# Queries, keys and the two merge gates of a transformer layer: seven products of quadrants in the input projection instead of eight, with the gates taken out of the attention loop

## The chip, the core and the metric

The kernel runs on one core of a Trainium2 chip. A core has TensorE (PE in the profile: matmuls and transposes into PSUM), VectorE (DVE), ScalarE (ACT), GpSimd (POOL) and SyncE (SP), which issues most of the loads; ScalarE issues most of the stores. Each engine executes its own instructions in the order in which the program was scheduled and waits on semaphores for the others. The metric is device time of one execution in microseconds. Three executions of the kernel before took 2883.06 us in the median (2879.89 to 2885.41).

## What is computed

One layer over 1024 tokens of width 1024, with 256 context tokens, all in float32. This is the part that matters here:

```
p  = (x * (1 + sc1) + sh1) @ w_in              # 1024 x 1024  @  1024 x 11264
qr, kr, vr, gr, qd, kd, vd, gate_r, gate_d = split(p)
qr, kr, qd, kd = rope(qr), rope(kr), rope(qd), rope(kd)
y_ret = retention_readout(retention(qr, kr, vr), gr) @ w_ret_out
y_dif = diff_readout(diff_attention(qd, kd + context, vd + context)) @ w_diff_out
y_mix = (sigmoid(gate_r + b) * y_ret + sigmoid(gate_d + b) * y_dif) @ w_o
x     = layer_norm(alpha * x + g1 * y_mix)
... conv feed-forward, layer_norm
```

The four of `qr`, `kr`, `qd`, `kd` are 1024 columns each; `gate_r` and `gate_d` (the merge's two gates) are 1024 columns each; `gr`, the retention's own gate, is 2048. `kr` and `kd` are also computed for the context tokens. `diff_attention` has eight heads, two softmaxes each.

## The kernel before, in words

**Numbers.** Every float32 operand is split into a high part `h` (a cast to the rounded format fp32r on ScalarE) and a low part `l` (the rest, a subtraction on VectorE): `split`, line 84. A product of two such operands is three matmuls, h·h, h·l and l·h (`mm3`, line 245), each 128 x 128 weights against up to 512 columns. Weights come in through a ring of tiles (`load_split`, `w_cols`): raw, then `wh` and `wl`.

**Projection.** The modulated input lies transposed in SBUF as `xH`, `xL` (8 row blocks of 128 by 1024 tokens). `qd`, `kd`, `vd`, `qr`, `kr`, `vr` are produced in that order. For queries and keys one tile is 256 weight columns, that is two halves of 128 (`proj_dif`, `proj_ret`): each half is 8 row blocks x 3 matmuls x 2 cuts of 512 tokens = 48 matmuls, so 96 per tile (`proj_T`), and for keys another 24 of 256 columns per half for the context (`pcx`). There are 16 such tiles, 4 each of `qd`, `kd`, `qr`, `kr`; the first is done with the two halves side by side while the input is still being prepared (`proj_first`). The two halves are the pair that the rotary embedding combines: four multiplications from PSUM on VectorE, one subtraction and one addition on GpSimd (`rope`). For `qd` and `kd` the result is split again and goes to memory in 16 pieces of 32 partitions, issued by ScalarE. `vd` and `vr` are produced the other way round (tokens on partitions, `proj_N`).

**Attention.** 64 steps, one for each head and block of 128 queries (`steps`). Each step has two scores (`score`): 6 matmuls into the one PSUM tile `sp` (bufs=1), a scan on VectorE that scales, copies and takes the maximum (line 720), and an exponential on ScalarE. `combine` joins the two on VectorE (line 77), `flip` transposes the result on TensorE (`tp`, ten transposes) and splits it (`ath`, `atl`), and `avd` multiplies by the values every second step (`po`, 30 matmuls). Since `sp` is one tile, the next score cannot start before the scan of the last one has ended. Between the scores the generator `gates` (line 677) puts in work that depends on none of this: the projections of `gr` and of the two merge gates, 32 blocks of 128 columns, 48 matmuls each (`pg`), handed out in quarters of 12 matmuls. One quarter follows every score but the last of every sixteenth step (line 801); what remains is done after the last score.

**After it.** Retention, the merge (which reads the gates from `d_ga`), the output projection, the feed-forward network. The first of its two large products, `w_up`, is already done with seven products of quadrants in place of eight: 84 matmuls and their sums for each `f` (`first_products`, `product`, the loop at line 1350). The order of all instructions on each engine is set by a scheduler, which starts from the order of the program.

## Time and profile before

| | |
|---|---|
| median of three executions | 2883.06 us |
| the profiled execution | 2888.07 us, its span 2886.3 us |
| TensorE busy | 2793.8 us (97% of the span), 13610 matmuls |
| VectorE busy | 1626.6 us (56%) |
| ScalarE busy | 1122.6 us (39%) |
| GpSimd busy | 809.8 us (28%) |
| moved by DMA | 340 MB, mean 118 GB/s |

The profiled execution lies 5 us over the median. Busy matmuls overlap in the profile (a 512-column matmul shows 0.39 us, the next one starts 0.23 us after it), so the pace of TensorE is read from starts, or from the chain that ended last. That chain is 81% TensorE; the largest of its parts are `pg` (18%), `pxn` (11%) and `px` (11%). The granted TensorE clock is full nearly throughout.

### The profile page before, as it was taken

The numbers are of one execution on the slowest core, as the hardware profiler recorded it, in microseconds if no ns is written. First come the engines' busy times: TensorE is split into PE (matmuls) and PEld (weight loads), VectorE is DVE, ScalarE is ACT, GpSimd is POOL, SyncE is SP. The second block draws the span as 40 slices with busy tenths as digits, with TensorE's granted clock in tenths as the row PEclk, the third lists the DMA queues.
The fourth block names the chain that finished last, engine by engine and source line by source line (L and its number), as shares of the span: only waits on it lengthen the run. The fifth ranks groups of instructions, "written<-read, shape, count | busy, mean of one in ns | idle before, by whom it ended". The sixth has DMA issues, their size and how long they took to land.

```text
span 2886.3 us, 34740 instructions
## 1 busy us (share of the span) xinstructions
PE 2793.8 (97%) x13610; PEld 2327.8 (81%) x13610; DVE 1626.6 (56%) x2139; ACT 1122.6 (39%) x1570; POOL 809.8 (28%) x613
## 2 busy tenths in 40 slices
PE   7999999999999999999998999899998999999997
PEld 5888888888788888888886877788776788888876
DVE  4864243322167766777758775333556555557666
ACT  4321211111144545544546767433345444444221
POOL 3321022100000000000027764234442333337744
PEclk9999999999999999999999999999999999999999
DMA  8755332453233332323233433643321322224421
GB/s 250 212 165 168 125 124 79 132 175 110 70 92 92 112 95 93 108 91 103 65 113 107 140 115 113 236 150 120 118 89 52 110 81 88 81 81 168 138 95 59
DMA packets 261476, 340.18 MB, mean 118 GB/s; under 512 B 15479, under 2 KB 192064, under 8 KB 261312
## 3 DMA queue, kind: packets, MB, share of 16 engines
q1 hardware_dynamic: 222992, 258.50, 28.7%
q10 hardware_dynamic: 38320, 79.46, 7.8%
q8 instruction: 107, 1.75, 0.3%
q14 instruction: 57, 0.47, 0.1%
HBM read 242.73 MB, written 95.17 MB: 117 GB/s over the span
## 4 chain that ended last, share of the span: by engine, by line
PE 81%; DMA 5%; DVE 5%; POOL 3%; ACT 3%; issue 3%; SPq 0%; ACTq 0%; DVEq 0%; POOLq 0%
PE pg L253 18%; PE pxn L253 11%; PE px L253 11%; PE pu L253 8%; PE py L253 8%; PE pyd L253 6%; PE sp L717 5%; PE po L253 4%; PE pxo L253 2%; PE tp L741 2%; PE pcx L253 2%; DMA g<-d_gT 1%; DVE acc L71 1%; PE pS L253 1%; DMA wraw<-in_w_in 1%
## 5 line engine op out<-in xcount | busy, mean ns | idle before, releaser
L71 DVE TENSOR_TENSOR wl<-wraw,wh 128x1024 fp32r<-128x1024 f32 (+1 forms) x233 | 319.8, 1386 | 248.1 <-ACT wh L85 241.5
L85 ACT CAST wh<-wraw 128x1024 fp32r<-128x1024 f32 (+1 forms) x233 | 218.7, 947 | 473.0 <-PE pu L253 107.9
L71 POOL TENSOR_TENSOR rd<-ident,wh 128x512 fp32r<-128x512 f32 x16 | 18.2, 1137 | 860.6 <-ACT wh L85 827.0
L720 DVE TENSOR_SCALAR_CACHE_REDUCE e<-sp 128x1280 f32<-128x1280 f32 x128 | 190.5, 1489 | 107.2 <-PE sp L717 106.5
L82 ACT ACTIVATE e<-e,m 128x1280 f32<-128x1280 f32 x128 | 175.0, 1367 | 184.0 <-DVE e L720 183.6
L71 POOL TENSOR_TENSOR wraw<-wraw 128x512 f32<-128x512 f32 x85 | 148.9, 1752 | 266.7 <-DVE wl L71 254.3
L71 POOL TENSOR_TENSOR rp<-rp,rp 128x1024 f32<-128x1024 f32 x32 | 89.0, 2804 | 379.4 <-DVE rp L71 359.7
L253 PE MATMUL pg<-xH,wh 128*128 128x512 f32 x496 | 194.9, 393 | 0.0
L253 PE MATMUL pg<-xH,wl 128*128 128x512 f32 x496 | 194.7, 393 | 0.0
L253 PE MATMUL pg<-xL,wh 128*128 128x512 f32 x496 | 194.4, 392 | 0.0
L717 PE MATMUL sp<-ks,qd 128*128 128x512 f32 (+1 forms) x768 | 174.4, 362 | 1.5 <-DVE e L720 1.4
L253 PE MATMUL py<-opH,wh 128*128 128x512 f32 x384 | 150.9, 398 | 10.0 <-DVE ga L71 6.0
L253 PE MATMUL px<-xL,wh 128*128 128x512 f32 x512 | 158.2, 390 | 0.0
L253 PE MATMUL px<-xH,wl 128*128 128x512 f32 x512 | 157.7, 389 | 0.0
L253 PE MATMUL px<-xH,wh 128*128 128x512 f32 x512 | 156.8, 391 | 0.0
L253 PE MATMUL py<-opL,wh 128*128 128x512 f32 x384 | 152.1, 396 | 1.0 <-DVE opL L71 1.0
L253 PE MATMUL pxn<-wh,xH 128*128 128x512 f32 x384 | 151.1, 394 | 0.0
L253 PE MATMUL py<-opH,wl 128*128 128x512 f32 x384 | 150.8, 394 | 0.0
L253 PE MATMUL pxn<-wh,xL 128*128 128x512 f32 x384 | 149.6, 390 | 0.0
L253 PE MATMUL pxn<-wl,xH 128*128 128x512 f32 x384 | 149.4, 389 | 0.0
L717 PEld LDWEIGHTS sp<-ks,qd 128*128 128x128 f32 x768 | 129.3, 188 | 24.6 <-DVE e L720 4.2
L81 ACT ACTIVATE st<-pxn 128x1024 f32<-128x1024 f32 x30 | 30.8, 1027 | 235.0 <-PE pxn L253 231.0
(356 smaller groups left out, 7166.7 us busy)
## 6 DMA issues: line engine op xcount, KB each, us to landing
wraw<-in_w_in SPq DMA_DIRECT2D x88, 512.0 KB
wraw<-in_w_up SPq DMA_DIRECT2D x44, 512.0 KB
mr<-in_w_mod SPq DMA_DIRECT2D x32, 512.0 KB
qd<-d_qd SPq DMA_DIRECT2D x128, 128.0 KB
ga<-d_ga SPq DMA_DIRECT2D x24, 512.0 KB
d_u<-u SPq DMA_DIRECT2D x22, 512.0 KB
fl<-d_u SPq DMA_DIRECT2D x22, 512.0 KB
wraw<-in_w_down SPq DMA_DIRECT2D x22, 512.0 KB
```

The costliest lines, as they stand in the source:

```text
L71: eng.tensor_tensor(out=o, in0=a, in1=b, op=op)
L81: return S.activation(out=o, in_=a, func=func, bias=bias, scale=scale)
L82: return S.activation(out=o, in_=a, func=func, bias=bias, scale=scale, accum_out=accum)
L85: S.copy(out=h, in_=x)
L253: PE.matmul(ps[:, c:e], w, m[:, c:e], start=start and i == 0, stop=stop and i == 2, skip_group_check=more)
L717: st["pe"] = PE.matmul(sp[:, a:b], w, r["k"][c][:, a:b], start=part == 0, stop=part == 1).ins
L720: V.tensor_scalar(out=e, in0=sp[:, :TK], scalar1=-0.125, scalar2=None, op0=ALU.mult, op1=ALU.min, accum_out=m)
L741: PE.transpose(tp[:, k, :], a[:, k * P:(k + 1) * P], ident)
```

## The change

24 column tiles of 256 (the 16 of queries and keys, and 8 for the two merge gates) are laid out as 2 x 2 quadrants: weights by the two halves of the rows and the two halves of 128 columns, input by the two halves of the rows and the two halves of the tokens. Winograd's form of Strassen's scheme gives the tile with seven products of 4 row blocks x 3 matmuls instead of eight, 84 matmuls instead of 96. The first tile of `qd` keeps the old form, so 23 tiles have the new one. For this

- sums of the input's quadrants are made once, in float32, and split: three new pairs of operands (`xs`), and one that takes the place of a quadrant of `xH`/`xL`, whose old content is stored to memory (`d_a21`, 2 MB for both) and read back for `vd`;
- sums of the weights' quadrants are made for each tile on GpSimd (four subtractions of 128 x 512), and four tiles are split instead of two (`weights_1` to `weights_3`);
- results are put together in SBUF: four copies from PSUM on ScalarE and three additions on VectorE for each tile (`proj_pair`). The rotary multiplications read from SBUF afterwards;
- the context parts of `kd` are split and sent on their own, so a key tile of `kd` has 32 pieces to send instead of 16;
- `gates` in the attention loop has 16 blocks (`gr`) instead of 32, and a quarter follows only the first score of a step, and not in steps 7, 11 and 15 of 16. 53 quarters lie in the loop or ahead of it, 11 after the last score;
- the ring of weights has 4 pairs instead of 6, and `decays` (the small tables of the retention) moves from the second query tile to the start of `vd`.

```
-    open_ring("wring1", 3, 6)
+    open_ring("wring1", 3, 4)
...
+            if k < 4:
+                continue
+            j = k - 4
+            a11, a12, a21, a22 = xn[:, j, t_lo], xn[:, k, t_lo], xn[:, j, t_hi], xn[:, k, t_hi]
+            tt(a11, a11, a21, ALU.subtract, G)
+            split(xs[7][0][:, j, :], xs[7][1][:, j, :], a11)
+            tt(a21, a21, a22, ALU.add)
+            tt(a22, a22, a11, ALU.subtract)
+            split(xs[6][0][:, j, :], xs[6][1][:, j, :], a22)
+            tt(a12, a12, a22, ALU.subtract, G)
+            split(xs[3][0][:, j, :], xs[3][1][:, j, :], a12)
...
+        def rope(pa, pb):
+            u, v = [rp.tile([P, T], F32R, name="rt%d" % i, tag="rt%d" % i, bufs=2) for i in range(2)]
+            t0, t1, p0, p1 = [x.bitcast(F32) for x in (u, v, pa, pb)]
+            tt(t0, p0, trig["cos"], ALU.mult)
+            tt(t1, p1, trig["sin"], ALU.mult)
+            tt(p0, p0, trig["sin"], ALU.mult)
+            tt(p1, p1, trig["cos"], ALU.mult)
+            tt(t0, t0, t1, ALU.subtract, G)
+            tt(p0, p0, p1, ALU.add, G)
...
+        def weights_1(f):
...
+            W[f] = {"raw": raw, "h0": ring_split(raw[0], perm, None if ctx else (0,))}
+            tt(b11, b12, b11, ALU.subtract, G)
+            tt(b12, b22, b12, ALU.subtract, G)
+        def weights_2(f):
...
+            W[f]["h1"] = ring_split(raw[1], perm)
+            tt(b22, b22, in_order(raw[0], perm, 0), ALU.subtract, G)
+            tt(b21, b21, b22, ALU.subtract, G)
+            W[f]["t0"] = ring_split(raw[0], perm)
+        def weights_3(f):
+            W[f]["t1"] = ring_split(W[f]["raw"][1], todo[f][1])
...
+        def product(ps, f, n, first):
+            w, at = W[f][places[n][0]], places[n][1]
+            for k in range(4):
+                mm3(ps, [x[:, at + k * P:at + k * P + P] for x in w], operand(n, k), 512, first and k == 0, k == 3, more=not first)
+        def proj_pair(f):
...
+            product(chain, f, 1, True)
+            S.copy(out=a[:, t_lo], in_=chain)
+            product(p2, f, 2, True)
+            tt(a[:, t_lo], a[:, t_lo], p2, ALU.add)
+            product(chain, f, 6, False)
+            S.copy(out=b[:, t_lo], in_=chain)
+            product(p5, f, 5, True)
+            S.copy(out=b[:, t_hi], in_=p5)
+            product(chain, f, 7, False)
+            tt(b[:, t_hi], b[:, t_hi], chain, ALU.add)
+            if f + 1 < len(todo):
+                weights_1(f + 1)
+            product(p5, f, 3, False)
+            tt(b[:, t_lo], b[:, t_lo], p5, ALU.add)
...
+            product(chain, f, 4, False)
+            S.copy(out=a[:, t_hi], in_=chain)
...
+        rot, todo = todo[1:] + ret, todo[:1]
+        for i, x in enumerate(rot):
+            todo.append(x)
+            if gat and i % 2 == (i > 6):
+                todo.append(gat.pop(0))
...
-            todo += [(C_GA + i * P, d_ga[i // 8, i % 8]) for i in range(16)]
...
-                    if c == 0 or n % 16 != 15:
+                    if c == 0 and n % 16 not in (7, 11, 15):
```

TensorE in the attention loop, before, at the second half of a step: `sp` are the score's matmuls, `tp` the transposes, `pg` the gate's matmuls.

```order
L717 MATMUL sp<-ks,qd 128x512 x2
L717 MATMUL sp<-ks,qd 128x256
L717 MATMUL sp<-ks,qd 128x512 x2
L717 MATMUL sp<-ks,qd 128x256
L741 MATMUL tp<-ident,e 128x128 x10
L253 MATMUL pg<-xH,wh 128x512
L253 MATMUL pg<-xL,wh 128x512
L253 MATMUL pg<-xH,wl 128x512
L253 MATMUL pg<-xH,wh 128x512
L253 MATMUL pg<-xL,wh 128x512
L253 MATMUL pg<-xH,wl 128x512
L253 MATMUL pg<-xH,wh 128x512
```

The same engine in the changed kernel, at one of the steps without a quarter:

```order
L878 MATMUL tp<-ident,e 128x128 x10
L854 MATMUL sp<-ks,qd 128x512 x2
L854 MATMUL sp<-ks,qd 128x256
L854 MATMUL sp<-ks,qd 128x512 x2
L854 MATMUL sp<-ks,qd 128x256
L854 MATMUL sp<-ks,qd 128x512 x2
L854 MATMUL sp<-ks,qd 128x256
L854 MATMUL sp<-ks,qd 128x512 x2
L854 MATMUL sp<-ks,qd 128x256
L878 MATMUL tp<-ident,e 128x128 x10
L854 MATMUL sp<-ks,qd 128x512 x2
L854 MATMUL sp<-ks,qd 128x256
```

Here two scores follow each other with nothing between, and ten transposes stand alone between the next two.

ScalarE at two key tiles of `kd`, before: `dh` and `rp` are the high and low parts that are sent, `wh` the cast of weights.

```order
L85 CAST dh<-pcx 128x256
L85 CAST wh<-wraw 128x1024 x2
L85 CAST dh<-rp_1670 128x1024
L85 CAST dh<-pcx 128x256
L497 DMA d_kd<-dh 32x1280 x2
L497 DMA d_kd<-rp_1670 32x1280 x2
L497 DMA d_kd<-dh 32x1280
L497 DMA d_kd<-rp_1670 32x1280
L497 DMA d_kd<-dh 32x1280
L497 DMA d_kd<-rp_1670 32x1280
L85 CAST dh<-rp_1672 128x1024
L497 DMA d_kd<-dh 32x1280 x3
```

ScalarE at such a tile in the changed kernel; `pa`, `pb` are the tiles in which the result is put together, `cl`, `ch` the context's.

```order
L589 COPY pa<-px 128x512
L85 CAST wh<-wraw 128x512 x2
L85 CAST rt_1954<-rt_1953 128x1024
L593 COPY pb<-px 128x512
L497 DMA d_kd<-rt_1954 32x1024 x3
L497 DMA d_kd<-rt_1953 32x1024 x3
L497 DMA d_kd<-rt_1954 32x1024
L497 DMA d_kd<-rt_1953 32x1024
L85 CAST pb<-pa 128x1024
L595 COPY pb<-pg 128x512
L497 DMA d_kd<-pb 32x1024 x3
L497 DMA d_kd<-pa 32x1024 x3
```

Copies that TensorE's next products wait for now stand between the sends on this queue.

## Rows read from the trace of the kernel before

**Rows 1.** Engines by stage: start, queries/keys of retention, attention, the handover to retention.

```profile
core 0: us, PE busy (x) PEld busy (x) DVE busy (x) ACT busy (x) POOL busy (x), PEclk, DMA share, GB/s
0.00:86.60 86.60, 66.02 (x407) 50.29 (x408) 47.55 (x102) 34.35 (x54) 33.44 (x52) 0.98 0.79 239
359.40:556.80 197.40, 197.40 (x962) 167.25 (x962) 75.73 (x58) 19.97 (x25) 41.63 (x15) 1.00 0.29 98
787.00:1474.00 687.00, 684.77 (x3901) 595.30 (x3901) 480.64 (x716) 344.62 (x476) 16.08 (x14) 1.00 0.30 93
1474.00:1560.00 86.00, 72.59 (x347) 60.33 (x346) 60.37 (x88) 43.19 (x72) 54.17 (x34) 0.88 0.39 123
```

**Rows 2.** Chain that ended last (start, us, what): key tiles in the projection.

```profile
161.18 2.87 PE pcx L253 x24
164.05 10.91 PE px L253 x48
```

**Rows 3.** The same chain, two successive `f` of the product with `w_up`.

```profile
2409.62 5.06 PE pu L253 x22
...
2428.91 5.06 PE pu L253 x22
```

**Rows 4.** TensorE in the attention loop, in order of time (start, us, ...).

```profile
1004.42 1.25 PE L741 MATMUL tp<-ident,e 128*128 128x128 f32 x10
1005.43 1.41 PE L717 MATMUL sp<-ks,qd 128*128 128x512 f32 x6
1006.68 0.39 PE L253 MATMUL pg<-xH,wh 128*128 128x512 f32 x1
...
1009.43 0.28 PE L253 MATMUL po<-ath,vh 128*128 128x256 f32 x1
...
1013.02 1.32 PE L717 MATMUL sp<-ks,qd 128*128 128x512 f32 x6
1014.18 0.40 PE L253 MATMUL pg<-xH,wh 128*128 128x512 f32 x1
```

**Rows 5.** VectorE in the attention loop: the first and the last scan.

```profile
787.08 1.48 DVE L720 TENSOR_SCALAR_CACHE_REDUCE e<-sp 128x1280 f32<-128x1280 f32 x1
...
1474.06 1.49 DVE L720 TENSOR_SCALAR_CACHE_REDUCE e<-sp 128x1280 f32<-128x1280 f32 x1 [0.64 <-PE sp L717]
```

**Rows 6.** VectorE within a step (in brackets: idle before, and what ended it).

```profile
1019.44 1.22 DVE L71 TENSOR_TENSOR wl<-wraw,wh 128x1024 fp32r<-128x1024 f32 x1
...
1029.93 0.16 DVE L732 RECIPROCAL f<-s 128x1 f32<-128x1 f32 x1 [1.52 <-ACT e L82]
...
1030.43 1.55 DVE L77 SCALAR_TENSOR_TENSOR e<-e,f 128x1280 f32<-128x1280 f32 x1
1031.92 1.49 DVE L720 TENSOR_SCALAR_CACHE_REDUCE e<-sp 128x1280 f32<-128x1280 f32 x1
...
1033.34 1.49 DVE L71 TENSOR_TENSOR atl<-tp,ath 128x1280 fp32r<-128x1280 f32 x1
```

**Rows 7.** Who waited for whom from 787 to 1474 (us, times, longest).

```profile
DVE e L720 <- PE sp L717: 105.9, 68, 4.5
...
PE sp L717 <- DVE e L720: 1.4, 1, 1.4
```

**Rows 8.** TensorE after the last score.

```profile
1489.24 0.38 PE L253 MATMUL po<-ath,vh 128*128 128x256 f32 x1 [1.31 <-ACT ath L85]
...
1491.12 1.08 PE L854 MATMUL pt<-ident,kraw 128*128 128x128 f32 x4 [1.50 <-DMA kraw<-d_kr]
```

**Rows 9.** TensorE's busy time and granted clock in two stretches of the handover.

```profile
1490.00:1500.00 10.00, 8.88 (x45) 0.66 0.82 245
1520.00:1530.00 10.00, 7.02 (x34) 0.72 0.47 143
```

**Rows 10.** GpSimd and VectorE: two of each at once in the projection, and GpSimd elsewhere.

```profile
217.64 5.76 POOL L71 TENSOR_TENSOR rp<-rp,rp 128x1024 f32<-128x1024 f32 x2 [21.81 <-DVE rp L71]
...
218.72 5.75 DVE L71 TENSOR_TENSOR wl<-wraw,wh 128x1024 fp32r<-128x1024 f32 x2
...
2036.32 2.40 POOL L71 TENSOR_TENSOR wraw<-wraw,mrow 128x1024 f32<-128x1024 f32 x1 [7.02 <-issue]
...
2318.82 2.68 POOL L71 TENSOR_TENSOR wraw<-wraw 128x512 f32<-128x512 f32 x2 [4.53 <-DVE wl L71]
```

**Rows 11.** ScalarE's queue in the projection: three sends of a key tile.

```profile
202.75 1.26 ACTq L497 DMA_DIRECT2D d_kd<-dh  x3
```

More of the change, by code (lines that the diff above doesn't have):

```diff
@@ L435, in build @@
     with ExitStack() as ph:
[L436 to L438 removed]
+        wp = wp1
         trig = {}
@@ L481, in proj_dif @@
[L481 to L493 removed]
+            return px
@@ new lines, in build, with ring_split @@
+        W = {}
+        def ring_split(raw, perm, only=None):
+            pair = [ring["pool"].tile([P, 1024], F32R, name="w" + n, tag="w" + n, bufs=ring["bufs"]) for n in "hl"]
+            if perm or only is not None:
+                for s in range(2) if only is None else only:
+                    c = slice(512 * s, 512 * s + 512)
+                    split(as_raw(pair[0][:, c], perm), as_raw(pair[1][:, c], perm), in_order(raw, perm, s))
+            else:
+                v = raw.rearrange("p (a s c) -> p s a c", a=4, s=2)
+                split(*[x.rearrange("p (s a c) -> p s a c", s=2, a=4) for x in pair], v)
+            return pair
@@ new lines, in build @@
+        rot, todo = todo[1:] + ret, todo[:1]
[3 more added lines that the diff above has]
+                todo.append(gat.pop(0))
+        first = proj_first(ws0)
+        with tc.issue_after(turns["mod"]):
+            weights_1(1)
+            weights_2(1)
+            weights_3(1)
+        for i, x in enumerate((xH, xL)):
+            ST.dma_start(out=d_a21[i], in_=x[:, 0:4, t_hi].bitcast(F32))
+        for k in range(4):
+            split(xH[:, k, t_hi], xL[:, k, t_hi], xn[:, k, t_hi])
@@ L627, in build @@
+        p0x.close()
+        ropex = ExitStack()
+        rp = ropex.enter_context(tc.tile_pool(name="rope", bufs=1, side="right"))
         with tc.issue_after(turns["mod"]):
             trig_tables("dif")
-        for g in range(4):
-            with tc.issue_after(turns["mod"]) if g == 1 else ExitStack():
-                proj_dif(C_QD, g, d_qd, False)
-            if g == 0:
-                with tc.issue_after(turns["mod"]):
-                    context()
-            if g == 1:
-                decays()
@@ L637, in build @@
-        for g in range(4):
-            proj_dif(C_KD, g, d_kd, True)
+        pair0 = out_tiles()
+        for o, p in zip(pair0, first):
+            S.copy(out=o.bitcast(F32), in_=p)
+        finish_dif(0, d_qd, pair0, None)
+        for f in range(1, len(todo)):
+            if todo[f][0] == C_QR:
+                trig_tables("ret")
+            proj_pair(f)
+            if f == 2:
+                context()
+        for i, x in enumerate((xH, xL)):
+            SP.dma_start(out=x[:, 0:4, t_hi].bitcast(F32), in_=d_a21[i])
```

160 lines of the change are left out of this document (98 added, 62 removed).

## The prediction

> **What bounds the kernel now.** I read the engines by stage first, then the chain that ended last, then the order of time on TensorE and VectorE inside the attention loop. In queries and keys TensorE is busy for all of 197.4 us, and in the attention loop for 684.8 of 687.0 us [rows 1]. The chain there is one matmul after the other: 48 of 512 columns in 10.91 us, 0.2273 us each, and 2.87 us for the 24 of a context part [rows 2]. So TensorE's pace sets the time in both stages that the change touches, and fewer matmuls count in full only where nothing else takes TensorE's place. In queries and keys VectorE is at 38% and ScalarE at 10%, so there is room. In the loop VectorE is busy for 480.6 us of 687 [rows 1], and while TensorE waits for its scan 1.4 us in all, VectorE waits 105.9 us for scores [rows 7]. The gate quarters are what keeps TensorE full there: each is 2.75 us (1006.68 to 1009.43) between scores of 1.16 us (1013.02 to 1014.18) [rows 4].
>
> **The change, part by part.** All sums are made against the profiled execution (2888.07 us, its span 2886.3) and then put on the median, which is 5 us lower.
>
> *Rotary tiles.* A tile costs 96 x 0.2273 = 21.82 us now. What 84 matmuls of the new form cost is in the trace: the product with w_up has the same seven products with the same copies and additions, and its period is 2428.91 - 2409.62 = 19.29 us [rows 3]. That is 2.53 us less, and 15 tiles have it: -38.0 us. The context parts stay as they are.
>
> *Gates in the projection.* Eight tiles of 19.29 us are new there: +154.3 us.
>
> *Gates out of the loop.* 16 blocks of 48 matmuls leave it, 64 quarters. At 2.75 us that would be 176 us, if TensorE stayed the bound, but it doesn't. I took the order of the changed kernel and went through the 127 intervals between one score and the next, on TensorE and VectorE, with durations from [rows 4, 6]: a score 1.16 us, a quarter 2.75, ten transposes 1.01 (1004.42 to 1005.43), thirty value matmuls 3.59 (1009.43 to 1013.02); a scan 1.42 (1031.92 to 1033.34), the combination 1.49 and 0.5 for its factor (1029.93 to 1031.92), the split of the transposed tile 1.4 to 1.5, of weights 1.22, and 0.2 to 1.0 for the small steps of values and read-out. An interval lasts as long as the longer of the two, and never less than a scan and a score in turn, 2.85 us, since the scores share one PSUM tile. For the order of before this gives 692 us (97 intervals by TensorE, 30 by VectorE). The trace has 1474.06 - 787.08 = 687.0 us [rows 5], so the accounting holds within 1%. For the order of the changed kernel it gives 576 us: 52 intervals are set by TensorE (270 us), 72 by VectorE (298 us, in which TensorE has 199 us of work), 3 by the pair of scan and score. TensorE's own sum is 474 us, VectorE's 478: nearly equal, and because each waits for the other at every score, the sum of the longer ones is 100 us above either. 75 intervals have no quarter; 48 of them have less than 2.85 us of work for TensorE, mostly just ten transposes. The loop shortens by 687 - 576 = 111 us, not by 176: -111.
>
> *The rest of the gates.* 11 quarters stand after the last score, 3 before the change: 8 x 2.75 = +22.0 us. They cover the waits of 1.31 and 1.50 us there [rows 8] and some of the time at a lower clock behind them (0.66 from 1490 to 1500 [rows 9]): -4. Together +18.
>
> *The start.* The input's sums add 12 casts, 20 VectorE and 8 GpSimd operations of 512 columns before the first new tile, and 2 MB are stored (8 to 9 us of transfer at 239 GB/s) where DMA is already 79% busy. TensorE has 66.0 of 86.6 us of work there, VectorE 47.6, GpSimd 33.4 [rows 1]. Most of it fits beside the loads. Between -2 and +15, I take +4. The read-back of 2 MB stands ahead of one weight load on SyncE's queue, but waits only for the fifth product of the last tile, with some 11 us of matmuls behind it: 0.
>
> *Waits in the new tiles.* Each tile has four copies and three additions that the product after next needs, so an engine that is late by more than 2.7 us stops TensorE. A rotary tile of `qd` has about ten VectorE operations with both operands in SBUF (1.22 us each) and 10 us on GpSimd: four of 128 x 512 (2.68 for two) and two of 128 x 1024 (2.40 each) [rows 6, 10]. Two such operations of each, side by side, took from 217.64 to 224.47, 6.8 us, where one after the other they need 7.2 [rows 10]. They hardly overlap. So the two engines need about 24 us for a `qd` tile, 22 for a `qr` tile and 12 for a gate tile, against 19.3 on TensorE (25 for keys); two rotary tiles and a gate tile come to 60 against 58. And ScalarE issues 32 sends per `kd` tile at 0.42 us [rows 11], between copies that TensorE waits for. In the w_up stage none of this shows, because there VectorE multiplies nothing for the rotation. Between 0 and +40, I take +12, half a microsecond a tile, nearer to the w_up row than to the full serial sum because the scheduler puts context matmuls into the gaps.
>
> The Trainium skill (SBUF — State Buffer, section "Who interferes with whom") says that a VectorE instruction with two SBUF inputs and a GpSimd instruction that reads SBUF exclude each other for the whole instruction. The 6.8 us agree with it. It speaks against the change, since the rotary multiplications read PSUM before and SBUF after; by it alone the sum would be the rival below on the projection.
>
> *The clock.* In the handover TensorE, with gaps of 1 to 2 us, fell to 0.66 and 0.72 of its clock, a mixture of 1.2 and 2.4 GHz [rows 9]. The 72 intervals in which TensorE waits have gaps of about the same size. At 0.72 its 199 us there become 276, still under the 298 that VectorE needs in total, but not in each interval. Between 0 and +40, I take +8.
>
> *The sum.* -38.0 + 154.3 - 111 + 18 + 4 + 12 + 8 = +47.3 us: 2935 for a profiled execution, 2883 + 47 = **2930 us** for the median, 1.6% slower. Per matmul the change is right (276 fewer, 63 us). What it loses is the cover in the loop, where a gate matmul cost its 0.23 us and kept nothing waiting; taken out, a sixth of the loop is waiting instead.
>
> **The rivals.**
>
> *Faster: the loop stays TensorE's.* If VectorE ran ahead and every wait were filled, the loop would end at TensorE's own 474 us, 102 us earlier: 2828 us. The change is faster once the loop is below 529 us (687 less 154.3 - 38.0 + 18 + 24 = 158), or below 553 with the three unknown costs at nothing. For it: VectorE had 106 us of waits for scores to give back [rows 7]. Against it: its own work without the 16 splits is still 461 us, a scan can't start before its score, and every score waits for the scan before it. The accounting would have to be 23 to 47 us wrong, where it was 5 us too high on before. 8%.
>
> *The clock falls throughout the loop.* If TensorE runs at 1.2 GHz in all waiting intervals, their 199 us become 398 against VectorE's 298, +100. About half of that is what the two stretches of the handover suggest: +50 in place of 8, 2972 us. For it: gaps of the same length did lower it [rows 9]. Against it: over the whole handover, 16% idle, the mean was still 0.88 [rows 1]. 13%.
>
> The Trainium skill (TensorE: Matmul & The Clock Gate, section "A second HAM failure mode: psum-queue depth-cycling") tells of a kernel in which short idle times between groups of matmuls let the clock swing between its two levels. The stretch from 1490 to 1530 shows such swings, the full loop of before does not.
>
> *The projection is set by VectorE, GpSimd and ScalarE.* If the serial sums above hold for `qd` and `qr` (3 tiles by 5 us, 4 by 2.5 us) and `kd`'s sends cost 4 us a tile, it is +40 in place of 12: 2958 us. 10%.
>
> *No difference.* The loop ends near 545 us and the unknown costs are small: 2883 us. 5%.
>
> **How the numbers follow.** The forecast, +15 to +75 us by the bounds of its unknown terms, has 64%; with the two slower rivals it is slower in 87%. Faster 8%, same 5%; about 0.2% is what a measurement of this kernel can tell from no change. For the range, the low end is the sum with the unknown costs at nothing and the loop 10 us shorter (+13, 2896), taken to 2894; the high end is +95 from all of them near their upper bounds, 2976. That leaves out the faster rival, no difference and the tail of the clock.
>
> **What would show it.** In the profile after: the loop from first to last scan at 570 to 595 us, with PE waiting for the scan at line 857 by some 80 us or more and VectorE above 75% busy. New tiles at 19.3 us in the chain (25 for keys), the whole of queries, keys and gates near 115 us longer than before. TensorE's total 63 us of pace lower while the span grows. If the clock is the matter, the loop shows a granted clock under 0.9. If the loop is under 550 us, the accounting by intervals is wrong and so is the sign; if the tiles take 21 us or more, the projection's other engines were priced too low.

## The result: 3.6% slower, twice the forecast loss

| | before | after |
|---|---|---|
| median | 2884.01 us (4 runs) | 2988.03 us (4 runs, 2985.72 to 2989.66) |
| ratio | | 1.0363, 95% interval 1.0345 to 1.0380 |
| span of the profiled execution | 2886.3 us | 2987.9 us |
| matmuls | 13610 | 13334 |

The forecast was 2930 (2894 to 2976): the sign was right, the time lies above the range. From the page of the changed kernel: busy time, the span in 40 slices, and the chain that ended last.

```profile
PE 2789.6 (93%) x13334; PEld 2294.9 (77%) x13334; DVE 1761.0 (59%) x2289; ACT 1208.3 (40%) x1711; POOL 980.0 (33%) x713
...
PE   6789999999999989898988999899998999999997
...
POOL 4554445410000000000004776313543233336753
PEclk8899999999999999999998999999999999999999
...
PE 56%; DVE 10%; DMA 4%; issue 4%; POOL 4%; ACT 3%; SPq 0%; ACTq 0%; DVEq 0%; POOLq 0%
```

TensorE has 276 matmuls less and is busy as long as before. The chain can be followed back only to 568.6 us here, over 81% of the span, so its 56% for TensorE can't be set against the 81% of before, where the chain covers everything. Slices lower than before stand in two places: the first three (the start and the first tiles; in two of them the granted clock is low as well) and from the 15th to the 22nd (the loop and the handover behind it). Where the 101.6 us went is read from three marks in the trace: the first matmul `pxn` of `vd`, the first scan and the last (start, us).

```profile
633.98 0.39 PE L254 MATMUL pxn<-wh,xH 128*128 128x512 f32 x1
```

```profile
984.63 1.48 DVE L857 TENSOR_SCALAR_CACHE_REDUCE e<-sp 128x1280 f32<-128x1280 f32 x1
...
1565.27 1.49 DVE L857 TENSOR_SCALAR_CACHE_REDUCE e<-sp 128x1280 f32<-128x1280 f32 x1 [1.31 <-PE sp L854]
```

Before, `vd` stood between `kd` and `qr`: the tiles took 0 to 246.7 and 359.4 to 556.8, 444.1 us together, and the values the rest up to 787.1.

| stage | before | forecast | after | difference |
|---|---|---|---|---|
| start and all tiles | 444.1 | +132.3 (-38.0 + 154.3 + 4 + 12) | 634.0 | +189.9 |
| values, up to the first scan | 343.0 | 0 | 350.7 | +7.7 |
| loop, first to last scan [rows 5] | 687.0 | -111 + 8 (clock) | 580.6 | -106.4 |
| behind the last scan | 1412.2 | +18 | 1422.6 | +10.4 |

So the loop came within 4 us of its sum and the tail within 8. The first row alone is 57.6 us over its sum, where the whole miss is 54.3. By stage, as [rows 1]: the start, the tiles of `qd` and `kd`, later tiles, the loop.

```profile
core 0: us, PE busy (x) PEld busy (x) DVE busy (x) ACT busy (x) POOL busy (x), PEclk, DMA share, GB/s
0.00:86.60 86.60, 56.01 (x331) 39.56 (x331) 60.15 (x103) 35.85 (x57) 43.41 (x59) 0.89 0.66 205
100.00:340.00 240.00, 208.41 (x953) 170.39 (x952) 148.93 (x146) 77.75 (x128) 114.04 (x60) 0.94 0.44 124
350.00:550.00 200.00, 196.68 (x896) 162.20 (x895) 108.56 (x94) 60.17 (x82) 94.27 (x50) 1.00 0.36 117
984.63:1565.27 580.64, 521.76 (x3067) 446.20 (x3066) 456.60 (x699) 308.92 (x424) 15.63 (x14) 0.98 0.25 79
```

The second of these stretches in the kernel before:

```profile
100.00:340.00 240.00, 240.00 (x1147) 200.11 (x1146) 128.62 (x181) 55.05 (x88) 37.62 (x14) 1.00 0.55 168
```

From 350 us on TensorE is busy for 98% at full clock: there a tile goes at its pace. Between 100 and 340 us it is idle for 32 us of 240 and its clock is at 0.94, where before it was busy throughout at full clock. The waits of TensorE there (us, times, longest) name above all ScalarE's copies of lines 589 to 595, which empty the PSUM that a tile's next product needs:

```profile
PE px L254 <- ACT pa L589: 16.1, 3, 7.7
PE px L254 <- ACT pb L593: 6.1, 2, 3.8
PE px L254 <- ACT wh L85: 3.4, 2, 3.0
PE pg L254 <- ACT pb L595: 3.2, 2, 2.4
```

One of these stops in order of time, TensorE and then ScalarE:

```profile
328.85 0.28 PE L254 MATMUL pcx<-cH,wl 128*128 128x256 f32 x1
336.39 0.80 PE L254 MATMUL px<-x6h,wh 128*128 128x512 f32 x1 [7.26 <-ACT pa L589]
336.99 0.63 PE L254 MATMUL px<-x6l,wh 128*128 128x512 f32 x1
337.41 0.63 PE L254 MATMUL px<-x6h,wl 128*128 128x512 f32 x1
```

```profile
330.03 4.71 ACTq L497 DMA_DIRECT2D d_kd<-rt  x8
334.79 1.04 ACT L85 CAST pb<-pa 128x1024 fp32r<-128x1024 f32 x1 [5.06 <-DMA d_kd<-rt]
334.81 0.42 ACTq L497 DMA_DIRECT2D d_kd<-ch  x1
335.28 0.43 ACTq L497 DMA_DIRECT2D d_kd<-cl  x1
335.75 0.58 ACT L589 COPY pa<-px 128x512 f32<-128x512 f32 x1
```

The copy at 335.75 stands behind ten sends; after 7.26 us of idle time the matmuls start 0.43 us apart, half of the full pace (1.2 in place of 2.4 GHz). To have one number for both, I reckon TensorE's **arrears**: the time less the sum of all matmuls started so far, each at its full pace (0.2273 us for 512 columns [rows 2], 0.1195 for 256, 0.1 for a transpose [rows 4]). Such a value is good to 1 or 2 us.

| arrears at (us) | 40 | 100 | 340 | end of the tiles |
|---|---|---|---|---|
| before | 20.0 | 21.2 | 22.8 | 23.1 |
| after | 26.4 | 43.4 | 90.0 | 101.1 |

The change loses 22 us more than before in the start and 56 from there to the end of the tiles, against 4 and 12 in the sum.

### The profile page after: what moved, and what is told of

Read it like the earlier page. It is cut to its first block, busy times and chain, and to the rows that moved or that the text cites. A ratio compares the mean times of both kernels' runs of the same rounds, so it can differ in the third digit from the quotient of the medians.

```text
span 2987.9 us, 34837 instructions
## 1 busy us (share of the span) xinstructions
PE 2789.6 (93%) x13334; PEld 2294.9 (77%) x13334; DVE 1761.0 (59%) x2289; ACT 1208.3 (40%) x1711; POOL 980.0 (33%) x713
## 4 chain that ended last, share of the span: by engine, by line
PE 56%; DVE 10%; DMA 4%; issue 4%; POOL 4%; ACT 3%; SPq 0%; ACTq 0%; DVEq 0%; POOLq 0%
PE pg L254 11%; PE pxn L254 9%; PE pu L254 8%; PE py L254 7%; PE pyd L254 6%; PE po L254 4%; PE sp L854 3%; DVE e L857 2%; PE pxo L254 2%; PE tp L878 2%; PE pS L254 1%; DVE atl L71 1%; DVE e L77 1%; PE px L254 1%; DMA mr<-in_w_mod 1%
## 5 line engine op out<-in xcount | busy, mean ns | idle before, releaser
L71 DVE TENSOR_TENSOR wl<-wraw,wh 128x1024 fp32r<-128x1024 f32 (+1 forms) x290 | 356.5, 1244 | 269.0 <-ACT wh L85 260.1
L71 POOL TENSOR_TENSOR wraw<-wraw 128x512 f32<-128x512 f32 x177 | 298.1, 1684 | 502.3 <-DVE wl L71 486.3
L85 ACT CAST wh<-wraw 128x1024 fp32r<-128x1024 f32 (+1 forms) x290 | 261.1, 914 | 450.2 <-PE pu L254 106.8
L854 PE MATMUL sp<-ks,qd 128*128 128x512 f32 (+1 forms) x768 | 181.4, 373 | 41.8 <-DVE e L857 41.7
L254 PE MATMUL pg<-xH,wh 128*128 128x512 f32 x424 | 167.6, 395 | 0.7 <-ACT sg L833 0.7
L254 PE MATMUL pg<-xH,wl 128*128 128x512 f32 x424 | 166.5, 393 | 0.8 <-DVE wl L71 0.8
L254 PE MATMUL pg<-xL,wh 128*128 128x512 f32 x424 | 166.5, 393 | 0.0
L81 ACT ACTIVATE st<-pxn 128x1024 f32<-128x1024 f32 x30 | 30.7, 1024 | 203.5 <-PE pxn L254 194.6
L85 ACT CAST ath<-tp 128x1280 fp32r<-128x1280 f32 x64 | 78.4, 1225 | 82.2 <-PE tp L878 82.2
L71 DVE TENSOR_TENSOR atl<-tp,ath 128x1280 fp32r<-128x1280 f32 x64 | 95.2, 1488 | 23.1 <-ACT ath L85 22.7
L77 DVE SCALAR_TENSOR_TENSOR e<-e,f 128x1280 f32<-128x1280 f32 x64 | 99.2, 1550 | 1.5
L71 POOL TENSOR_TENSOR sl<-S,sh 128x512 fp32r<-128x512 f32 x64 | 91.6, 1440 | 16.0 <-ACT sh L85 12.5
```

What stands on the lines that cost most here:

```text
L71: eng.tensor_tensor(out=o, in0=a, in1=b, op=op)
L77: V.scalar_tensor_tensor(out=o, in0=a, scalar=s, in1=b, op0=op0, op1=op1)
L81: return S.activation(out=o, in_=a, func=func, bias=bias, scale=scale)
L85: S.copy(out=h, in_=x)
L254: PE.matmul(ps[:, c:e], w, m[:, c:e], start=start and i == 0, stop=stop and i == 2, skip_group_check=more)
L854: st["pe"] = PE.matmul(sp[:, a:b], w, r["k"][c][:, a:b], start=part == 0, stop=part == 1).ins
```

## The experiments

All are edits of the changed kernel. A median stands beside that of the kernel before on the same chip (2882 to 2885); "first scan" is the time of the loop's first scan, 787.1 before and 984.6 after.

### What the rotary part and the gates cost apart

Gates back in the loop, no gate tiles:

```
-        NP = 8
+        NP = 0
             todo = [(C_GR + i * P, d_gT[i]) for i in range(16)]
+            todo += [(C_GA + i * P, d_ga[i // 8, i % 8]) for i in range(16)]
-                    if c == 0 and n % 16 not in (7, 11, 15):
+                    if c == 0 or n % 16 != 15:
```

> The rotary part alone: the changed kernel with no gate tiles in the projection, the 32 blocks of gates back in the attention loop and handed out as before. By the terms of the forecast: 15 x 2.53 = 38.0 less, start +4, waits +8, nothing in the stage of the values: about 2858. By the trace of the changed kernel: TensorE fell behind its pace by 20 us more than before at the start, by 47 us between 100 and 340 us, by 10 us in the stage of the values; nearly all of it lies in tiles of qd and kd and so stays without the gate tiles: 2884 - 38 + 20 + 47 + 10, 2910 to 2925. If the gate tiles themselves were what is crowded, it comes below 2890. The loop is back at 680 to 690 us.

2928.32 us, ratio 1.0158 (1.0139 to 1.0177). The tiles end at 486.9, 42.8 us later than before where the sum had 22 less; the loop takes 684.3. So the miss is in the rotary part: 65 us of it without a single gate tile. The eight gate tiles cost 634.0 - 486.9 = 147.1 us, 18.4 each: less than the 19.29 of [rows 3], probably because they give the rotary tiles time. A wait of the context appears that the gate tiles had covered:

```profile
PE ptc L661 <- POOL xc L74: 21.8, 1, 21.8
```

Half of the gates: four tiles, eight blocks in the loop:

```
-        NP = 8
+        NP = 4
+            todo += [(C_GA + i * P, d_ga[0, i]) for i in range(8)]
-                    if c == 0 and n % 16 not in (7, 11, 15):
+                    if c == 0 or n % 2 == 0:
```

> The changed kernel with four gate tiles in the projection and the other gate (8 blocks of 128 columns) in the attention loop; there a quarter follows the first score of each step and the second of every second step, 96 quarters. The accounting by intervals of the forecast, on the order of this kernel, gives 647 us from the first to the last scan (87 intervals by TensorE, 40 by VectorE; TensorE's own sum 593, VectorE's 489). Rivals: TensorE's own sum, 593; a straight line between 580.6 (16 blocks) and 684.3 (32 blocks), 632. Total about 2980 by the accounting, since four gate tiles of 18 to 19 us leave the projection.

One execution, 2932.13 us. The loop takes 627.9, not 647. TensorE shows as busy for 98% of it:

```profile
897.80:1525.70 627.90, 616.09 (x3592) 533.61 (x3590) 471.06 (x709) 331.08 (x456) 15.85 (x14) 1.00 0.29 90
```

```profile
PE sp L855 <- DVE e L858: 8.8, 14, 1.6
```

The accounting had 54 us lost (647 - 593). In the trace the loop's matmuls, each at its full pace, come to 594 us, and 32 are lost; the 12 us in which no matmul shows as busy are less than that, since busy records overlap. The straight line (632) was nearest. The first eight blocks taken out give 56 us of loop and cost 63 us of tiles (550.0 - 486.9); the second eight give 47 and cost 84. The second step loses clearly. The first loses 7 us by these stages and 4 in the total, which one execution doesn't tell from nothing.

### GpSimd beside VectorE

All sums of the tiles on VectorE (`tt(..., G)` becomes `tt(...)`):

```
-            tt(b11, b12, b11, ALU.subtract, G)
+            tt(b11, b12, b11, ALU.subtract)
...
-            tt(t0, t0, t1, ALU.subtract, G)
-            tt(p0, p0, p1, ALU.add, G)
+            tt(t0, t0, t1, ALU.subtract)
+            tt(p0, p0, p1, ALU.add)
```

> The changed kernel, but the sums of weight quadrants (four of 128 x 512 a tile) and the two sums of the rotation are on VectorE, so GpSimd does nothing in the tiles. Theory P (port): the two engines exclude each other, each GpSimd sum of 128 x 512 takes 1.68 us of both and would take 0.68 on VectorE alone; a rotary tile needs some 6 us less of the two together, and the 47 us between 100 and 340 us shrink by 25 or more: 2965 or less. Theory S (sends on ScalarE's queue): the copies stand where they stood, 2980 to 2990. If VectorE becomes the bound of the tiles the time rises above 2995.

2950.26 us, 1.0234 (1.0214 to 1.0254): 38 us less, first scan 947.1. VectorE's busy time between 100 and 340 us, this run:

```profile
100.00:340.00 240.00, 222.00 (x1043) 183.66 (x1042) 163.66 (x212) 85.18 (x140) 7.69 (x10) 0.97 0.46 135
```

VectorE does 66 operations more and is busy for 14.7 us more (163.66 against 148.93), while GpSimd loses 106 us of work (7.69 against 114.04). The other operations became shorter; the split of weights from 100 to 600 us, in the changed kernel and in this run (mean ns of one behind the comma):

```profile
L71 DVE TENSOR_TENSOR wl<-wraw,wh 128x1024 fp32r<-128x1024 f32 x49 | 75.7, 1553 | 37.5 <-ACT wh L85 30.3 <-issue 6.8
```

```profile
L71 DVE TENSOR_TENSOR wl<-wraw,wh 128x1024 fp32r<-128x1024 f32 x54 | 65.3, 1222 | 13.4 <-ACT wh L85 12.2
```

Arrears at 340 us are 66 instead of 90, and from there on they don't grow: the tiles are at TensorE's pace. The run doesn't part two ways in which it helps: VectorE is no longer held up, and each sum is itself shorter (a rotary sum of 128 x 1024 took 2.95 to 3.32 us on GpSimd and takes 1.22 on VectorE). The two kinds of sums apart:

```
-            tt(b11, b12, b11, ALU.subtract, G)
-            tt(b12, b22, b12, ALU.subtract, G)
+            tt(b11, b12, b11, ALU.subtract)
+            tt(b12, b22, b12, ALU.subtract)
```

> The changed kernel, but only the four sums of weight quadrants (128 x 512) of each tile are on VectorE; the two sums of the rotation (128 x 1024) stay on GpSimd. With both kinds on VectorE it was 2950, 38 us less than with both on GpSimd. Theory C (the chain of the rotation): the rotation's two sums lie between a tile's end and the freeing of its buffers, 3.3 us each on GpSimd beside a busy VectorE, and this is what makes the copies late; then this run gives less than half of the 38 us, 2970 or more. Theory W (weights): the sums of weights, 88 of 128 x 512 at 1.62 us, hold VectorE's splits and make the next tile's weights late; then it gives most of it, 2950 to 2960. If only the sum of GpSimd's time beside VectorE counts (the port), the two runs share the gain by GpSimd's time: weights 142.7 us of 240, so 23 us here, 2965.

2972.75 us, 1.0306 (1.0284 to 1.0328), first scan 970.2.

```
-            tt(t0, t0, t1, ALU.subtract, G)
-            tt(p0, p0, p1, ALU.add, G)
+            tt(t0, t0, t1, ALU.subtract)
+            tt(p0, p0, p1, ALU.add)
```

> The counterpart: only the rotation's two sums on VectorE, the weights' sums on GpSimd. Theory C: more than half of the 38 us, 2955 to 2965. Theory W: less than half, 2970 to 2985. By shares of GpSimd's time: rotation 97.4 us of 240, 15 us, 2973.

2970.08 us, 1.0294 (1.0272 to 1.0315), first scan 960.8. Against the ratio of the change (1.0363) the weights' sums give about 16 us and the rotation's about 20, and both at once gave 37: they add. Which of them gives more is not shown. The intervals overlap, and the first scans, 14.4 and 23.8 us earlier, are of single executions, this one 8 us below its median and the one before 5 us above. Each theory met one of its two ranges alone (C 2970 or more for the weights, but not 2955 to 2965 here; W 2970 to 2985 here, but not 2950 to 2960 for the weights), and a share by GpSimd's time (15 us here, 23 for the weights) is neither shown nor excluded.

### The sends

Sixteen pieces of 32 partitions joined to four transfers:

```
-                for i in range(4):
-                    for part, src in ((0, h), (1, l)):
-                        r0 = part * 64 + half * 32
-                        ST.dma_start(out=dst[4 * g + i, r0:r0 + 32, at:at + n], in_=src[32 * i:32 * i + 32, :n].bitcast(F32))
+                for part, src in ((0, h), (1, l)):
+                    r0 = part * 64 + half * 32
+                    ST.dma_start(out=dst[4 * g:4 * g + 4, r0:r0 + 32, at:at + n], in_=src[:, :n].bitcast(F32))
```

> The changed kernel, but the 16 pieces in which a tile of qd or kd goes to memory are joined to four transfers of 128 partitions (and likewise the 16 of the context part), so ScalarE issues 4 where it issued 16. Theory S (sends): TensorE's stops in the tiles of qd and kd, and the half clock behind them, come from the copies pa and pb that stand behind sends of about 0.43 us each on ScalarE's queue. Then most of the 47 us that TensorE falls behind its pace between 100 and 340 us goes away: 2988 becomes 2945 to 2960. Rival P (port): the stops come from VectorE and GpSimd holding each other up; the sends matter little, 2980 to 2990. Rival D (transfers): the copies wait for the landing of the same 1 MB, not for the issuing; then fewer and larger pieces change at most 10 us.

3069.77 us, 1.0649 (1.0628 to 1.0670): 82 us slower, outside every expectation. The copy waits for the buffer that the send holds (ScalarE, then the DMA engines' busy share in 40 slices of 0.625 us from 112 us on):

```profile
112.94 0.53 ACTq L496 DMA_DIRECT2D d_qd<-pa  x1
113.50 1.04 ACT L85 CAST wh<-wraw 128x1024 fp32r<-128x1024 f32 x1 [0.91 <-PE px L254]
135.84 0.59 ACT L588 COPY pa<-px 128x512 f32<-128x512 f32 x1 [21.29 <-DMA d_qd<-pa]
```

```profile
DMA  2222279957999932222222222222222221111000
```

The joined transfers of a tile, each with four as its outermost size, together keep some 0.2 of the 16 DMA engines busy at about 100 GB/s, and the last of them holds its tile for 21 us. The Trainium skill (DMA: Bandwidth & Descriptors, section "Why a DMA increments its semaphore by 16 and not by 1") says that the outermost size of a transfer's pattern limits how many of the engines take part; four of sixteen agrees with this row. The run shows that the landing of sends can stop a tile, but not what the issuing costs. Two runs for that; the pieces issued by SyncE:

```
-                        ST.dma_start(out=dst[4 * g + i, r0:r0 + 32, at:at + n], in_=src[32 * i:32 * i + 32, :n].bitcast(F32))
+                        SP.dma_start(out=dst[4 * g + i, r0:r0 + 32, at:at + n], in_=src[32 * i:32 * i + 32, :n].bitcast(F32))
```

> The changed kernel, but the pieces of qd and kd are sent by SyncE instead of ScalarE; their number and size stay. Theory I (issuing): the copies pa and pb are late because 16 to 32 sends at about 0.43 us stand ahead of them on ScalarE. Then TensorE loses 20 to 35 us less between 100 and 340 us: 2955 to 2970. Theory L (landing): the copies wait until the send of the tile two before them has left its buffer (in the run with joined sends one copy waited 21.3 us for that); who issues the sends matters little, 2978 to 2992, or slower where weight loads wait behind sends on SyncE's queue.

2987.95 us, 1.0362: no change. ScalarE's copies cost TensorE less (3.0 us for `pa` behind 130 us), but the context's wait grows to 11.2. And sent from a table that never changes, which frees the result tiles early:

```
-                        ST.dma_start(out=dst[4 * g + i, r0:r0 + 32, at:at + n], in_=src[32 * i:32 * i + 32, :n].bitcast(F32))
+                        ST.dma_start(out=dst[4 * g + i, r0:r0 + 32, at:at + n], in_=trig["cos" if part else "sin"][32 * i:32 * i + 32, :n])
```

> The changed kernel, but the pieces of qd and kd are sent out of the cosine and sine tables instead of the result (as many, as large, issued by ScalarE), so the queries and keys of the attention are not the computed ones; the results are split as before. No send holds a result tile or waits for a split now. Theory L (landing): the waits of ScalarE's copies for the result tiles go, 20 to 35 us less, 2955 to 2970. Theory I (issuing): the sends still take ScalarE's queue 0.43 us each, within 10 us of 2988. If both hold, this run and the one with SyncE share the gain. If neither changes anything, the chain of rotary sums alone is late, and only the run with these sums on VectorE (2950) touched the cause.

2974.78 us, 1.0328 (1.0303 to 1.0352): 13 us less, first scan 968.6. So the holding of the result tiles is worth 13 to 16 us here, together with the sends' own wait for the splits, which this edit takes away too. The issuing alone is worth nothing that shows in this kernel.

### Start and tables

The weights of the first new tile split after the last row block's cast:

```
-            split(xH[:, k, :], xL[:, k, :], xn[:, k, :])
+            turns["x"] = S.copy(out=xH[:, k, :], in_=xn[:, k, :]).ins
+            tt(xL[:, k, :], xn[:, k, :], xH[:, k, :].bitcast(F32), ALU.subtract)
...
-        with tc.issue_after(turns["mod"]):
+        with tc.issue_after(turns["x"]):
             weights_1(1)
```

> The changed kernel, but the weights of the first new tile are split after the cast of the input's last row block instead of beside the modulation. In the changed kernel the last row block's small steps on VectorE stand between eight splits and sums (its factor is ready at 84.9 us; the vector it is made from at 76.1), and TensorE waits 8.2 us for that block at 88.9. Theory O (order): the block comes some 6 to 8 us earlier, 2974 to 2984. Theory V (VectorE's total): VectorE has the same work ahead of the first new tile either way, which then starts as late, 2984 to 2994.

2990.34 us, 1.0369. TensorE waits 3.3 us for the block instead of 8.2, and then 7.2 for the weights; arrears at 100 us are about the same. That is what theory V, VectorE's total, had: 60 us busy in the first 86.6, 48 before [rows 1]. GpSimd's time grew there too (43 us against 33), and this run does not part the two.

The input's rows in the tiles of the later sums, so that the ring of weights is free for the modulation:

```
+            xb2 = xsp.tile([P, 2, D], F32, name="xb", tag="x%d%s" % ((6, 3)[b0 // 4], "hl"[b0 // 2 % 2]))
             for b in (b0, b0 + 1):
-                t = ring["pool"].tile([P, D], F32, name="xb", tag="wl" if b < 4 else "wraw" if b < 7 else "wh",
-                                      bufs=ring["raws"] if 4 <= b < 7 else ring["bufs"])
+                t = xb2[:, b - b0]
```

> The changed kernel, but the eight rows tiles of the input lie where the sums of the input come later, not in the ring of weights, which has 4 pairs here instead of 6. Theory R (ring): the first weights of the modulation are loaded late because their places in the smaller ring are held by input rows (the second load was issued at 28.1 us, before at 23.7, and TensorE waited 6.2 us for it); this is the first part of what the start lost, 20 against 26 us behind pace at 40 us. Then 4 to 10 us less: 2978 to 2984. Rival (VectorE's load decides when the first tile is done, whatever came before): 2985 to 2990.

2986.05 us, 1.0355 (1.0330 to 1.0381). The ring theory holds for the first 40 us (arrears 21.1 instead of 26.4, as before), but by 100 us 39.9 are left of 43.4 and the first scan is 2.3 us earlier: most of the time is lost again further on, as the rival had it.

The tables after the first half of `vd`:

```
-        decays()
         for g in range(2):
             proj_N(C_VD + g * 512, d_vd, g * 512, True, AF.Copy)
+            if g == 0:
+                decays()
```

> The changed kernel, but the small tables of the retention are made after the first half of vd instead of ahead of it. Theory T: between 640 and 730 us TensorE falls 10 us behind because the loads, casts and small VectorE work for the tables stand ahead of the weights of vd and of the vector md that TensorE's own queue waits for; the stop goes, 2975 to 2980. Rival: the stop comes from the reading back of the 2 MB that were stored (88% DMA share between 650 and 700 us) and the weights behind it; then nothing changes, 2984 to 2990.

2981.42 us, 1.0346 (1.0323 to 1.0368): 6.6 less, first scan 974.5. The stage of the values is back at 342.9, so its +7.7 is the moved step, which the sum had at 0.

### Towards a rotary part that pays

Gates in the loop, all sums on VectorE, tables later (the edits above), and the context a tile later:

```
-            if f == 2:
+            if f == 3:
                 context()
```

> The rotary part alone (gates in the attention loop), with the sums of weights and rotation on VectorE, the retention's tables after the first half of vd, and the context prepared one tile later. From the run with the gates in the loop (2928): sums on VectorE saved 38 us with the gate tiles between, here 25 to 40; the tables 6; the wait of 21.8 us of TensorE's transposes of the context for GpSimd goes. 2928 - 30 - 6 - 20 = 2872, 2860 to 2885: the start (about 20 us) keeps it from 2846, which 15 x 2.53 us less than before would be. If VectorE, which then has all the sums and no gate tiles as relief, becomes the bound of the rotary tiles: 2895 or more.

2899.74 us, 1.0056 (1.0041 to 1.0071): outside the range expected; the context's wait did not go, it is 20.2 us. Then the tiles in another order:

```
-        rot, todo = todo[1:] + ret, todo[:1]
+        rot, todo = todo[1:4] + ret + todo[4:], todo[:1]
...
-            if f == 2:
+            if f == 5:
                 context()
```

> The rotary part alone (gates in the loop), sums on VectorE, tables after the first half of vd, and the tiles in another order: three of qd, four of qr, four of kr, four of kd, with the context prepared after the second qr tile. In the run before it (2900) TensorE waited 20.2 us for the context's normalised rows, whose buffer was held by the low part of a qd tile until it was sent; a qr tile does not send that buffer. Without that wait and the half clock behind it: 2870 to 2880, that is 0.1 to 0.5% faster than before (2882). If another wait takes its place (the tables of cosine and sine are loaded once more): 2890 or more.

2900.70 us, 1.0063 (1.0047 to 1.0079): the wait is 14.7 us and others take its place. Input rows as above, tables after the second half, and the context in two steps:

```
                 ts(t, t, rs[:, b:b + 1], cst[:, b, 0:1], ALU.mult, ALU.add, G)
+            yield
+            for b, t in enumerate(xb):
                 for i in range(2):
                     pt = small_ps("ptc").rearrange("p (k t) -> p k t", k=4)
...
-                context()
+                late = context()
+                next(late)
+            if f == 6:
+                next(late, None)
```

> The rotary part alone: gates in the loop, sums on VectorE, queries first, the tables after the second half of vd, input rows in the tiles of the sums, and the context in two steps, its loads and norms after the second qr tile, its transposes a tile later. From the run with queries first (2901): the context's wait of 14.7 us and the half clock behind it go, 15 to 20; the start 4 to 8; the tables 0 to 5: 2901 - 25 = 2876, 2868 to 2888. Below 2876 the seven products pay in queries and keys (0.2% under before); at 2885 or more the wait only changes its place, and the part's 38 us are spent on VectorE's extra work.

2904.66 us, 1.0072 (1.0058 to 1.0086): not better. The context's two waits are 7.4 and 4.9 us now, but the copies and casts behind the sends of `kd` cost more: one cast of weights for `vd` stops TensorE for 10.5 us. So the sends move to SyncE, by the same edit as above:

> As the run before, with the pieces of qd and kd sent by SyncE. In the run with queries first one copy stood behind ten sends of kd on ScalarE (3.7 us of TensorE, and the half clock). Issuing theory: 3 to 8 us less than the run before, 2868 to 2874. Rival: weight loads behind sends on SyncE's queue give it back, within 3 us of it or slower.

2888.70 us, 1.0018 (1.0010 to 1.0027): 16 us less than the run before, twice the expected gain. The same edit gave nothing in the changed kernel, where GpSimd's sums make the results late; that this is the reason is not shown, since the two kernels differ in more. What is left of the context (GpSimd):

```profile
208.72 6.79 POOL L74 TENSOR_SCALAR cn<-cn,aff 128x256 f32<-128x256 f32 x4 [2.71 <-ACT cn L664]
220.36 2.18 POOL L74 TENSOR_SCALAR cn<-cn,aff 128x256 f32<-128x256 f32 x4 [4.84 <-ACT cn L664]
```

The same kind of four operations, first beside VectorE's rotary multiplications, then with VectorE idle. They go to VectorE, and the first two sections of `mods` leave the first half of each part of `vd`:

```
-                    ts(cn[i][:, j, :], cn[i][:, j, :], aff[:, 0, 1, k:k + 1], aff[:, 1, 1, k:k + 1], ALU.mult, ALU.add, G)
+                    ts(cn[i][:, j, :], cn[i][:, j, :], aff[:, 0, 1, k:k + 1], aff[:, 1, 1, k:k + 1], ALU.mult, ALU.add)
...
-                if b % 4 == 0:
+                if b % 4 == 0 and (c0 != C_VD or b == 8):
                     next(fill, None)
```

> As the run before, with two edits: the factor and shift of the context's rows (four operations of 128 x 256 twice) on VectorE instead of GpSimd, and the first two of the sixteen vector sections made in the stage of the values are skipped there and made later. In the run before (2888.7) four of those operations took GpSimd 6.79 us beside a busy VectorE, against 2.18 us for the next four while VectorE was idle; ScalarE's cast and copy stood behind them, and TensorE waited 10.5 us. If GpSimd and VectorE hold each other up (the port), that wait and the half clock go: 10 to 14 us, and 0 to 8 for the second edit: 2870 to 2880, which is below before (2884). If the wait was for a buffer, it stays: 2885 to 2890.

2878.71 us (11 runs), 0.9985 (0.9973 to 0.9997): below the kernel before, but by 0.15%, less than the 0.2% that I call a difference. The context's wait is still 8.2 us (10.5 in the run before), so most of it was not GpSimd; the gain is in the values, where arrears no longer grow (55.3 at 460 us, 57 at 640), which points to the second edit. Arrears at 100 us are 34.0, at 340 us 54.8; before 21.2 and 22.8. Of the 38 us of fewer matmuls, 32 are eaten by then: 13 in the start and 19 in the tiles behind it, about half of these by the context's wait and the clock behind it. Some of these edits (the sends above all) might help the kernel before as well; that wasn't tried.

```profile
PE 2761.5 (96%) x13430; PEld 2296.0 (80%) x13430; DVE 1731.8 (60%) x2349; ACT 1195.6 (42%) x1697; POOL 728.4 (25%) x581
```

## Why the forecast was right in sign and wrong in size

- **Rotary tiles, -38.0:** right as a pace, not as a time. Between 350 and 550 us the new tiles run at it (98% busy), and with the sums on VectorE at all of it. In the change the part alone costs +42.8 at the end of the tiles. So the forecast's sign is right by the gates alone: their move cost 60 us (2988 - 2928, the sum had 69), while the rotary part, with start and waits 22 us faster in the sum, was 44 us slower (2928 - 2884).
- **Waits in the new tiles, +12 (0 to 40): the step that failed.** It measured 56 (arrears from 100 us to the end of the tiles, less the 1.9 of before), beyond its bound. The row that said so was on the list [rows 10], and the serial sum of the two engines was made from it; but I took a value near the `w_up` row, "because the scheduler puts context matmuls into the gaps". The part of GpSimd's sums beside VectorE is shown: with all sums on VectorE the tiles end 35 us earlier, and behind 100 us arrears grow by about 26 us instead of 58. Where these 26 come from is open; the sends may be part of it, but the two edits were not tried together in this kernel. The bound fell short because it left out the half clock behind the longer stops (between 100 and 340 us arrears grow by 47; TensorE is idle for 32 of them, the other 15 are the clock) and the result tiles, which sends hold (13 to 16 us). The rival "the projection is set by VectorE, GpSimd and ScalarE" was the mechanism of these waits, with 10%, and its 2958 was still 30 us short.
- The Trainium skill (SBUF — State Buffer, section "Who interferes with whom") was cited for two-input VectorE instructions; the split's mean of 1553 ns in the stage with GpSimd's sums and 1222 without them agrees.
- **The start, +4 (-2 to +15):** 22. About five at 40 us are the smaller ring, of which two are left at the first scan; that the rest is VectorE's total ahead of the first new tile is what the two runs on the start leave over, not something that a run took away. I had called it hidden "beside the loads". My count of operations also left out four casts and four subtractions of 512 columns, by which the fourth pair takes the quadrant's place, and I had no term for the clock there (0.89, before 0.98).
- **Gates in the projection, +154.3:** 147.1.
- **The loop, -111, and the clock, +8:** -106.4. The accounting had 474 us of TensorE's own work and 102 lost. In the trace the loop's matmuls, each at its full pace, come to 476 us, and 103 are lost (the 522 us that show as busy hold the drawn-out ends of matmuls and the slower clock as well). What TensorE waits for is not quite what I had named: it is idle for 59 us, 41.7 for the scan of line 857 where I had 80, 10.8 for the combination, the rest small. That the sum fits so well is partly luck: on the order with half of the gates the same accounting has 54 us lost where the trace has 32, and it is 19 us too high. That it lets no engine catch up in the next interval is a likely reason, not a shown one.

```profile
PE sp L854 <- DVE e L857: 41.7, 46, 3.1
PE tp L878 <- DVE e L77: 10.8, 19, 1.0
```

- **Values and read-back, 0:** +7.7, of which the tables are 6.6; I had listed their move and priced only the read-back. **Rest of the gates, +18:** +10.4.
- The clock did not fall throughout the loop (0.98); it fell in the start (0.89) and in the tiles (0.94), where I had looked for none.
- Of the signs that I had named, the loop's 570 to 595 us (580.6) and VectorE's share above 75% (79%) came; queries, keys and gates near 115 us longer did not (189.9).

## What to carry to other kernels

Fewer matmuls pay only if the copies, sums and splits that replace them fit beside TensorE on engines that don't hold each other up: add VectorE and GpSimd into one sum where both read SBUF, and where that sum is near TensorE's, take it as the least price (here it was still 30 us short), not a value near a stage in which VectorE had less to do. Independent work that fills a dependent loop should be moved out only if its new place costs less than the loop gets shorter; here each half lost. A long stop of TensorE cost its length and the half clock behind it, and removing one showed the next, so price a step by what is late second.

## What the runs showed of the hardware

- A multiplication of VectorE that reads PSUM is not slowed by GpSimd, a split with both operands in SBUF is. In the kernel before, from 100 to 600 us, the means are 1217 ns and 2194 ns. Half of the multiplications by the cosine had a GpSimd sum beside them and took 1214 ns, the others 1221; the 18 splits with one beside them took 2840 ns, the 12 without 1224. In the change the multiplications read SBUF and take 1447 to 2080 in the mean.

```profile
L71 DVE TENSOR_TENSOR wl<-wraw,wh 128x1024 fp32r<-128x1024 f32 x30 | 65.3, 2194 | 45.4 <-ACT wh L85 44.4
L71 DVE TENSOR_TENSOR rp<-px,cos 128x1024 f32<-128x1024 f32 x29 | 35.3, 1217 | 46.2 <-PE px L253 46.2
```

- With joined transfers of 4 x 32 x 1024 a copy waited 21 us for its tile. With the same bytes in pieces of 32 x 1024, in the changed kernel, it could start 7.4 us after the first piece was issued and 3.7 after the last (ScalarE):

```profile
114.00 1.38 ACTq L497 DMA_DIRECT2D d_qd<-pa  x3
...
117.70 0.31 ACTq L497 DMA_DIRECT2D d_qd<-pa  x1
...
121.36 0.59 ACT L589 COPY pa<-px 128x512 f32<-128x512 f32 x1 [1.25 <-DMA d_qd<-pa]
```

- Between 100 and 340 us of the changed kernel each of the six stops of TensorE from 2.35 to 7.67 us was followed by a stretch at 1.2 GHz (granted clock 0.50 to 0.64 in the 4 us behind it); two of 0.98 and 1.14 us were not. In the loop, with 59 us of idle time in stops of up to 3.15 us, the mean stays at 0.98.
